# Seven block products per pair of weight units in the output and down projections of a transformer-style layer

## The chip, the cores and the metric

The kernel runs on one core of a Trainium2 chip. The core's engines work side by side: TensorE (PE, with PEld for its weight loads), VectorE (DVE), ScalarE (ACT), GpSimd (POOL) and SyncE (SP, which issues the DMAs). The time is that of one execution in device microseconds; a profile of one execution is read beside it.

## What is computed

One layer of a hybrid encoder runs over 512 prompt tokens and 32 sample tokens (544 in all, T in the code), model width 1024. Cut to the part that matters here:

```python
gate_a, gate_b = jnp.split(jax.nn.sigmoid(gates + b_gate), 2, axis=-1)
x = x + (gate_a * (ya @ w_proj_a) + gate_b * (yb @ w_proj_b)) @ w_out
u = rmsnorm(x, g_ffn) @ w_up                       # 1024 -> 2 x 3072
ug, uv = jnp.split(causal_dwconv(u_ext, ffn_conv_w, ffn_conv_b), 2, axis=-1)
x = x + (jax.nn.gelu(ug, approximate=True) * uv) @ w_down      # 3072 -> 1024
x = x + jax.nn.sigmoid(rmsnorm(x, g_ple) @ w_ple_gate) * (pe @ w_ple)
```

## The kernel before, in words

Activations lie with features on the 128 partitions and the 544 tokens along the row. All dense products run as one list of steps (`dense_steps`); TensorE takes them in exactly that order, since `Ordered` ties each matmul to the one before. The other engines' queues are ordered by the framework's scheduler.

A **unit** is a weight block of 1024 inputs by 128 outputs, 192 of them. Two units come in one 1 MB DMA (`load`, a ring of two buffers `wr`). `prep` splits a unit for the matmul: ACT rounds it to `wh` (L250), DVE subtracts to get the rest `wl` (L254; POOL does it for some of the first 40 units). Activations are split in the same way into `hi` and `lo`. A **chunk** (`mm3`) is one of a unit's eight input blocks: wh by hi, wh by lo, wl by hi, each on both halves of 272 tokens, 6 matmuls. A unit is 48 matmuls. Its result lies in a pair of PSUM banks (`dps`, two such pairs), and an epilogue on DVE and ACT takes it away.

The steps from the end of the gates on: `pb` (8 results of two units, the second branch), `out` (8 units), `up` in three parts of 16 units, `down` in three parts of 8 units, `pw` (8 small products), `gate` (8 units). The order is up, up, down, up, down, down, pw, gate. `ep_out` adds a unit's product to the residual `x[m]` on DVE (L1011), splits the sum for the next step (`split_g`, L374, L375) and adds its squares to `acc` (`add_sq`, L383, L384); `ep_down` does so too in the last part. From `acc`, `sum_parts` (L388, L389) and `rstd_of` make the norm's factor: matmuls `rps` with a matrix of ones, put off by some chunks (`defer`), then ACT. `conv_up` is the epilogue of an `up` unit: three DVE evictions, one ACT and two DVE operations, and two tiny POOL copies; `ep_uv` multiplies the two halves into `me` and splits it.

Matmuls, DVE and ACT operations appear under a helper's line (L130 for every matmul).

## Time and profile before

| | us |
|---|---|
| median of 3 runs | 1357.71 (1355.65 to 1357.8) |
| profiled execution, its own time | 1355.77 |
| span of its trace | 1354.1 |

The span is the time from the first to the last instruction; 1.7 us of the execution lie around it. Busy time of an engine includes the time in which an instruction has been started and is held up.

### The profile page before, as it was taken

To read this page: it belongs to the slowest core of one execution; us is meant where nothing else is said; L and a number is where in the kernel's file an instruction comes from. 1 tells how busy PE (TensorE), PEld (TensorE's weight loads), DVE (VectorE), ACT (ScalarE), POOL (GpSimd) and SP (SyncE) were. 2 spreads that over 40 slices of the span, in tenths; PEclk is the share of its full clock that TensorE was granted. 3 is DMA by queue.
4 is the path that set the end of the run, shared out by engine and by line. 5 is a ranking of instruction groups with operands and counts; after the bars stand their busy time and mean duration, and the time that the engine had idled before them with its cause. 6 is when DMAs were issued, how large, how long until landed. Compare 5 with 4: busy or idle time off the path is not lost.

```text
span 1354.1 us, 26563 instructions
## 1 busy us (share of the span) xinstructions
PE 1338.2 (99%) x11045; PEld 1307.2 (97%) x11045; DVE 852.6 (63%) x1474; ACT 634.4 (47%) x1104; POOL 313.7 (23%) x442
## 2 busy tenths in 40 slices
PE   8999999999999999999999999999999999999998
PEld 7999998999999999999999999999999999999998
DVE  7999889755775656643554335677676356753545
ACT  5465555656676667542442223534444124432342
POOL 5456365544321211100000000133332013310000
PEclk9999999999999999999999999999999999999999
DMA  5733243332533332222223422222222232222231
GB/s 182 252 100 130 83 128 121 119 132 100 177 94 114 115 111 90 67 81 94 69 89 110 143 94 73 85 94 94 94 72 85 94 111 94 76 85 94 94 107 53
DMA packets 41896, 142.15 MB, mean 105 GB/s; under 512 B 9216, under 2 KB 13232, under 8 KB 29488
## 3 DMA queue, kind: packets, MB, share of 16 engines
q1 hardware_dynamic: 41776, 140.45, 31.4%
q8 instruction: 87, 1.43, 0.4%
q14 instruction: 33, 0.27, 0.1%
HBM read 129.27 MB, written 14.31 MB: 106 GB/s over the span
## 4 chain that ended last, share of the span: by engine, by line
PE 89%; DVE 6%; ACT 2%; DMA 1%; issue 1%; SPq 0%; POOL 0%; ACTq 0%; DVEq 0%; POOLq 0%
PE dps L130 80%; PE O L130 2%; PE yps L130 2%; PE L L130 1%; PE st L130 1%; DVE cv L599 1%; DVE qs L834 1%; PE Tp L133 1%; DVE wl L254 1%; PE xst L133 0%; PE gps L130 0%; DMA wr<-in_w 0%; DVE xs L603 0%; DMA ab<-asc 0%; PE qn L130 0%
## 5 line engine op out<-in xcount | busy, mean ns | idle before, releaser
L130 PE MATMUL dps<-hi,wh 128*128 128x272 f32 x2960 | 627.0, 293 | 0.6 <-DVE ext L574 0.4
L130 PE MATMUL dps<-lo,wh 128*128 128x272 f32 x2960 | 613.1, 288 | 4.1 <-DVE lo L375 4.1
L130 PE MATMUL dps<-hi,wl 128*128 128x272 f32 x2960 | 612.1, 288 | 0.0
L130 PEld LDWEIGHTS dps<-hi,wh 128*128 128x128 f32 x2960 | 466.0, 189 | 10.5 <-issue 7.8
L130 PEld LDWEIGHTS dps<-lo,wh 128*128 128x128 f32 x2960 | 465.9, 189 | 5.0 <-DVE lo L375 5.0
L130 PEld LDWEIGHTS dps<-hi,wl 128*128 128x128 f32 x2960 | 464.9, 188 | 0.0
L250 ACT CAST wh<-wr 128x1024 fp32r<-128x1024 f32 x192 | 201.2, 1048 | 386.0 <-PE dps L130 346.6
L254 DVE TENSOR_TENSOR wl<-wr,wh 128x1024 fp32r<-128x1024 f32 x173 | 213.6, 1235 | 47.6 <-ACT wh L250 42.3
L1033 DVE SCALAR_TENSOR_TENSOR ucv<-uext,vec,ucv 128x546 f32<-128x546 f32 x96 | 75.3, 784 | 4.4 <-ACT ucv L1030 2.7
L599 DVE SCALAR_TENSOR_TENSOR cv<-ext,hv,cv 128x547 f32<-128x547 f32 x72 | 71.0, 986 | 2.1 <-ACT cv L596 1.0
L1026 POOL COPY cfo<-uext 128x2 f32<-128x2 f32 x48 | 10.4, 217 | 261.7 <-DVE uext L573 261.7
L1023 POOL MEMSET uext<- 128x2 f32 x48 | 4.5, 95 | 278.7 <-issue 278.7
L1065 DVE TENSOR_TENSOR x<-x,dps 128x544 f32<-128x544 f32 x24 | 17.3, 721 | 78.0 <-PE dps L130 78.0
L571 DVE TENSOR_TENSOR uext<-dps,rstd 128x272 f32<-128x272 f32 x48 | 21.3, 443 | 63.0 <-PE dps L130 58.3
L785 DVE CUSTOM_DVE_ANT_0 P<-L,bias 128x128 f32<-128x128 f32 (+3 forms) x64 | 30.8, 481 | 46.1 <-PE L L130 41.6
L254 POOL TENSOR_TENSOR wl<-wr,wh 128x1024 fp32r<-128x1024 f32 x19 | 48.4, 2549 | 43.9 <-ACT wh L250 42.4
L1027 POOL COPY cfo<-uext 128x2 f32<-128x2 f32 x48 | 55.5, 1157 | 0.0
L787 ACT ACTIVATE P<-P,sm 128x128 f32<-128x128 f32 (+3 forms) x64 | 36.0, 562 | 26.8 <-DVE sm L785 26.4
L660 POOL TENSOR_TENSOR ab<-ab,bc 128x512 f32<-128x512 f32 (+1 forms) x28 | 37.0, 1325 | 40.7 <-ACT ab L659 40.7
L368 ACT CAST hi<-me 128x544 fp32r<-128x544 f32 x24 | 15.5, 647 | 61.9 <-DVE me L1051 61.9
L1030 ACT ACTIVATE ucv<-uext,vec 128x546 f32<-128x546 f32 x48 | 40.7, 847 | 7.2 <-DVE uext L574 2.6
L650 ACT ACTIVATE m<-ab,tm 128x128 f32<-128x128 f32 x128 | 40.8, 389 | 6.3 <-DMA ab<-asc 6.2
(243 smaller groups left out, 1548.9 us busy)
## 6 DMA issues: line engine op xcount, KB each, us to landing
wr<-in_w SPq DMA_DIRECT2D x96, 1024.0 KB, 4.9
ab<-asc SPq DMA_DIRECT2D x32, 256.0 KB, 5.1
bsc<-evec SPq DMA_DIRECT2D x16, 320.0 KB, 8.0
bias<-bsc SPq DMA_DIRECT2D x16, 256.0 KB, 3.2
xin<-in_xT SPq DMA_DIRECT2D x8, 272.0 KB, 5.7
out_o_v<-v SPq DMA_DIRECT2D x8, 272.0 KB, 3.2
out_o_k<-qk SPq DMA_DIRECT2D x8, 272.0 KB, 2.9
x<-in_xT SPq DMA_DIRECT2D x8, 272.0 KB, 4.4
```

The source lines that it names most:

```text
L130: return self._pin(nc.tensor.matmul(*args, **kw))
L250: cp = S.copy(hi, r)
L254: eng.tensor_tensor(lo, r, hi.bitcast(F32), op=SUB)
L571: V.tensor_tensor(ext[:, n : n + HALF], ps[:, 0, :HALF], rstd[:, 0:HALF], op=MUL)
L599: V.scalar_tensor_tensor(y[:, :n], ext[:, j : j + n], hv[:, 24 * j + ti : 24 * j + ti + 1], y[:, :n], op0=MUL, op1=ADD)
L650: S.activation(m[:, i], ab[:Q, i], AF.Relu, scale=-1.0, bias=tm[:Q, 1, c, hd : hd + 1])
L660: G.tensor_tensor(ab, ab, cc[:, tk].unsqueeze(1).to_broadcast([128, H, Q]), op=MUL)
L785: V.tensor_tensor_reduce(out=P, in0=L, in1=B, scale=1.0, scalar=3e38, op0=ADD, op1=MIN, accum_out=nm[:n])
L787: S.activation(P, P, AF.Exp, scale=-1.0, bias=nm[:n], accum_out=sm[:n])
L1027: G.tensor_copy(cfo[:, i, 2:4], ext[:, UW - 2 : UW])
L1030: S.activation(y[:, :n], ext[:, 0:n], AF.Identity, scale=vec[:, V_FW + i : V_FW + i + 1], bias=vec[:, V_FB + i : V_FB + i + 1])
L1033: V.scalar_tensor_tensor(y[:, :n], ext[:, j : j + n], vec[:, V_FW + 48 * j + i : V_FW + 48 * j + i + 1], y[:, :n], op0=MUL, op1=ADD)
```

## The change

The `out` step and each of the three `down` parts (8 units each) are computed in four **pairs** of units. For a pair, weights, activations and result are cut into 2 by 2 blocks: weights by even and odd input blocks and by unit, activations by even and odd input blocks and by token half. Instead of the 8 block products of a pair, 7 are made, of sums and differences of the blocks. A block product is 4 input blocks of 3 matmuls, 12 matmuls; a pair is 84 matmuls where it was 96.

- `split7` (for two activation tiles): four differences on POOL of 272 columns, and six splits on ACT and DVE.
- `weight_sums` (for a pair): four sums and differences on POOL of 512 columns, into tiles `ws`.
- `prep_to`: weights are split in halves of 512 columns (one product's weights), two products to a tile; the ring of `wh` and `wl` has three tiles (it had two) from `pb` on.
- `product_out`: takes a product from PSUM and adds it to the blocks of the result that need it: one ACT copy, seven DVE and four POOL operations of 272 columns for a pair. The additions of squares move from DVE to POOL.
- `product`: the matmuls of one product; products 1 and 2, 6 and 7, and 5 and 3 share a pair of banks each, product 4 has a bank of its own.
- `dense_steps`: down 0 stands after the first 18 units of up, down 1 after 34, and down 2 after `pw`, directly ahead of `gate`.
- The host packs the weights of `w_out` and `w_down` with even input blocks first.

```diff
--- before.py
+++ after.py
...
-    p += [("pb", m) for m in range(8)] + [("out", m) for m in range(8)]
-
-    def up(t):
-        return [(n, i) for i in range(8 * t, 8 * t + 8) for n in ("ug", "uv")]
-
-    def down(t):
-        return [("down", t, m) for m in range(8)]
-
-    p += up(0) + up(1) + down(0) + up(2) + down(1) + down(2)
-    p += [("pw", m) for m in range(8)] + [("gate", m) for m in range(8)]
+    p += [("pb", m) for m in range(8)] + [("out", 0)]
+
+    def up(a, b):
+        return [(n, i) for i in range(a, b) for n in ("ug", "uv")]
+
+    p += up(0, 9) + [("down", 0)] + up(9, 17) + [("down", 1)] + up(17, 24)
+    p += [("pw", m) for m in range(8)] + [("down", 2)] + [("gate", m) for m in range(8)]
     return p
+
+
+SEVEN = [(p, n) for n in range(4) for p in (1, 2, 6, 7, 5, 3, 4)]
+NEW = ("pb", 0)
...
+    def weight_sums(j):
+        r = raws[j].rearrange("p u (k c) -> p (u k) c", c=512)
+        s = sums[j] = [slot(name="ws") for _ in range(4)]
+        s1, s2, s3, s4 = (t[:, 0:512] for t in s)
+        G.tensor_tensor(s1, r[:, 2], r[:, 3], op=ADD)
+        G.tensor_tensor(s2, s1, r[:, 0], op=SUB)
+        G.tensor_tensor(s3, r[:, 0], r[:, 2], op=SUB)
+        G.tensor_tensor(s4, r[:, 1], s2, op=SUB)
+
+    def prep_to(n):
+        while len(prepped) < min(n, len(tiles)):
+            w = tiles[len(prepped)]
+            hi = pools["w2"].tile([128, 1024], F32R, tag="wh", name="wh", bufs=3)
+            lo = pools["w2"].tile([128, 1024], F32R, tag="wl", name="wl", bufs=3)
+            prepped.append((hi, lo))
+            if isinstance(w, int):
+                load(w // 2)
+                parts = [(None, None, slice(0, 1024), raws[w // 2][:, w % 2, :])]
+                load(w // 2 + 1)
+            else:
+                parts = []
+                for i, (p, j) in enumerate(w):
+                    load(j)
+                    if p == 1:
+                        weight_sums(j)
+                        if j - 1 not in sums:
+                            load(j + 1)
+                    r = raws[j].rearrange("p u (k c) -> p (u k) c", c=512)
+                    if p in (1, 2, 4):
+                        src = r[:, {1: 0, 2: 1, 4: 3}[p]]
+                    else:
+                        src = sums[j][{5: 0, 6: 1, 7: 2, 3: 3}[p]][:, 0:512]
+                    parts.append((p, j, slice(512 * i, 512 * i + 512), src))
+            for p, j, sl, src in parts:
+                S.copy(hi[:, sl], src)
+                V.tensor_tensor(lo[:, sl], src, hi[:, sl].bitcast(F32), op=SUB)
+                if p == 4:
+                    load(j + 2)
+                if p == 3:
+                    done(*sums[j])
...
+        def product(self, st):
+            if self.cur is None:
+                kp = acts_of[st[0]](st)
+                head = [(i, (0, 1, 2)) for i in range(3)] + [(i, (3,)) for i in range(3)]
+                self.cur = [0, kp, head + [(i, (0, 1, 2, 3)) for i in range(3, 28)], at[0], {}]
+            n, kp, todo, t0, banks = self.cur
+            i, ks = todo[n]
+            if i == 0 and ks[0] == 0:
+                prep_to(t0 + 2)
+            elif i >= 3:
+                prep_to(t0 + i // 2 + 3)
+            wh, wl = prepped[t0 + i // 2]
+            p, q = SEVEN[i]
+            if ks[0] == 0:
+                j = i % 7
+                if j in (0, 2, 4):
+                    banks["d"] = dps()
+                banks[p] = sps("dpb")[:, :HALF] if j == 6 else banks["d"][:, j % 2, :HALF]
+            b = banks[p]
+            for k in ks:
+                o = 512 * (i % 2) + 128 * k
+                xh_, xl_ = kp[k][p]
+                for m, (w, x_) in enumerate(((wh, xh_), (wh, xl_), (wl, xh_))):
+                    PE.matmul(b, lhsT=w[:, o : o + 128], rhs=x_, start=k == m == 0, stop=k == 3 and m == 2)
+            self.count += len(ks) / 2
+            if ks[-1] == 3:
+                product_out(st, p, q, b)
+            self.cur[0] += 1
+            if self.cur[0] == len(todo):
+                at[0] = t0 + 14
+                pos[0] += 8
+                self.cur = None
+                self.i += 1
+                epilogue[st[0]](*st[1:])
...
+    def split7(t0, t1, g=None):
+        ta, tb = eslot("ta"), eslot("tb")
+        b11, b12, b21, b22 = (t[:, s] for t in (t0, t1) for s in (slice(0, HALF), slice(HALF, T)))
+        c1, c2, c3, c4 = (t[:, s] for t in (ta, tb) for s in (slice(0, HALF), slice(HALF, T)))
+        G.tensor_tensor(c1, b12, b11, op=SUB)
+        G.tensor_tensor(c2, b22, c1, op=SUB)
+        G.tensor_tensor(c3, b22, b12, op=SUB)
+        G.tensor_tensor(c4, b21, c2, op=SUB)
+        ts = [slot(F32R, n) for n in ("bh", "bh", "bh", "bl", "bl", "bl", "bx")]
+        h = [t[:, s] for t in ts for s in (slice(0, HALF), slice(HALF, T))]
+        res = {1: (h[0], h[6]), 2: (h[1], h[7]), 3: (h[2], h[8]), 4: (h[3], h[9]), 5: (h[4], h[10]),
+               6: (h[5], h[11]), 7: (h[12], h[13]), 0: ts}
+        for hi, lo, src in ((*res[1], b11), (*res[2], b21), (ts[2], ts[5], ta[:, :T]), (*res[7], c3),
+                            (*res[3], b22), (*res[4], c4)):
+            if g is None:
+                S.copy(hi, src)
+                V.tensor_tensor(lo, src, hi.bitcast(F32), op=SUB)
+            else:
+                S.activation(hi, src, AF.Copy, scale=g)
+                V.scalar_tensor_tensor(lo, src, g, hi.bitcast(F32), op0=MUL, op1=SUB)
+        return res
...
-    def ep_out(ps, m):
-        V.tensor_tensor(h2(x[m]), h2(x[m]), pv(ps), op=ADD)
-        xh.append(split_g(x[m], vec[:, V_GFFN + m : V_GFFN + m + 1]))
-        add_sq(acc, x[m], m == 0, V)
-        if m == 7:
-            for p in mh:
-                done(*p)
-            sp2 = sum_parts(acc)
-            dense.defer(7, lambda: rstd_of(rstd, sp2, 1.0 / D, tanhs))
+    tmp = []
+
+    def product_out(st, p, q, b):
+        x11, x12, x21, x22 = (x[m][:, s] for m in (2 * q, 2 * q + 1) for s in (slice(0, HALF), slice(HALF, T)))
+
+        def add(eng, to, y):
+            eng.tensor_tensor(to, to, y, op=ADD)
+
+        if p == 1:
+            tmp[:] = slot(name="su"), slot(name="sv")
+            s1 = tmp[0][:, 0:HALF]
+            S.copy(s1, b)
+            add(G, x11, s1)
+        elif p == 2:
+            add(V, x11, b)
+        elif p == 6:
+            u = tmp[0][:, HALF:T]
+            V.tensor_tensor(u, tmp[0][:, 0:HALF], b, op=ADD)
+            add(G, x21, u)
+        elif p == 7:
+            add(V, x21, b)
+            add(V, x22, b)
+        elif p == 5:
+            v = tmp[1][:, 0:HALF]
+            V.tensor_tensor(v, tmp[0][:, HALF:T], b, op=ADD)
+            add(G, x22, v)
+            add(G, x12, v)
+            done(*tmp)
+        elif p == 3:
+            add(V, x12, b)
+        else:
+            add(V, x21, b)
+        if p == 4 and st != ("down", 0) and st != ("down", 1):
+            dst, v = (xh, V_GFFN) if st[0] == "out" else (xp, V_GPLE)
+            for m in (2 * q, 2 * q + 1):
+                dst.append(split_g(x[m], vec[:, v + m : v + m + 1]))
+                add_sq(acc, x[m], m == 0, G)
+
+    def ep_out(_):
+        for p in mh:
+            done(*p[0])
+        sp2 = sum_parts(acc)
+        dense.defer(7, lambda: rstd_of(rstd, sp2, 1.0 / D, tanhs))
...
+        if i % 2:
+            mid7[i // 2] = split7(mid[i - 1], me)
+            done(mid[i - 1], me)
...
+    def ep_down(t):
+        for i in range(4 * t, 4 * t + 4):
+            done(*mid7[i][0])
         if t == 2:
-            xp.append(split_g(x[m], vec[:, V_GPLE + m : V_GPLE + m + 1]))
-            add_sq(acc, x[m], m == 0, V)
-        if m == 7:
-            for i in range(8 * t, 8 * t + 8):
-                done(*mid[i])
+            sp2 = sum_parts(acc)
+            dense.defer(4, lambda: rstd_of(rstd, sp2, 1.0 / D, gelus))
```

How the queues change, at three places. POOL, from the end of the attention stage to the first `up` unit: before, nothing of the output projection is on this engine (`klz` and `acc` belong to the attention stage, `uext` and `cfo` to the first `up` unit).

```order
L835 TENSOR_TENSOR klz1_4430<-qk_6834,ks1_7346 64x512
L384 TENSOR_TENSOR acc_130<-acc_130,sq_7370 128x544
L384 TENSOR_TENSOR acc_130<-acc_130,sq_7482 128x544
L1023 MEMSET uext_10593 128x2
L1024 COPY uext_10593<-ctx_f_107 128x2
L1026 COPY cfo_109<-uext_10593 128x2
L1027 COPY cfo_109<-uext_10593 128x2
```

Now, inside the output projection, from the first pair's additions to the second pair's (`x_10109` and `x_10111` are the first pair's results, `su` and `sv` the shared sums, `ws` the third pair's weight sums, `wr` its raw weights):

```order
L1151 TENSOR_TENSOR x_10109<-x_10109,su_10157 128x272
L1151 TENSOR_TENSOR x_10111<-x_10111,su_10157 128x272
L1151 TENSOR_TENSOR x_10111<-x_10111,sv_10158 128x272
L1151 TENSOR_TENSOR x_10109<-x_10109,sv_10158 128x272
L267 TENSOR_TENSOR ws_10328<-wr_10188 128x512
L269 TENSOR_TENSOR ws_10330<-wr_10188 128x512
L268 TENSOR_TENSOR ws_10329<-ws_10328,wr_10188 128x512
L270 TENSOR_TENSOR ws_10331<-wr_10188,ws_10329 128x512
L515 TENSOR_TENSOR acc_133<-acc_133,sq_10270 128x544
L1151 TENSOR_TENSOR x_10113<-x_10113,su_10286 128x272
L1151 TENSOR_TENSOR x_10115<-x_10115,su_10286 128x272
L267 TENSOR_TENSOR ws_10455<-wr_10296 128x512
```

Between one pair's additions there now stand the four weight sums of the pair after next and the additions of squares. DVE in the output projection before: an eviction, the next unit's weight rest, the split, the squares.

```order
L1011 TENSOR_TENSOR x_10017<-x_10017,dps_10090 128x544
L254 TENSOR_TENSOR wl_10155<-wr_9959,wh_10154 128x1024
L375 SCALAR_TENSOR_TENSOR lo_10147<-x_10017,vec_76,hi_10146 128x544
L384 TENSOR_TENSOR acc_130<-acc_130,sq_10150 128x544
L1011 TENSOR_TENSOR x_10019<-x_10019,dps_10153 128x544
L254 TENSOR_TENSOR wl_10216<-wr_10095,wh_10215 128x1024
L375 SCALAR_TENSOR_TENSOR lo_10208<-x_10019,vec_76,hi_10207 128x544
L384 TENSOR_TENSOR acc_130<-acc_130,sq_10211 128x544
```

DVE now, from the last eviction of the first pair into the second pair (`dps` and `dpb` are products in PSUM):

```order
L1151 TENSOR_TENSOR x_10111<-x_10111,dpb_10247 128x272
L484 SCALAR_TENSOR_TENSOR lo_10262<-x_10109,vec_79,hi_10261 128x544
L484 SCALAR_TENSOR_TENSOR lo_10267<-x_10111,vec_79,hi_10266 128x544
L298 TENSOR_TENSOR wl_10291<-ws_10181,wh_10290 128x512
L298 TENSOR_TENSOR wl_10291<-wr_9974,wh_10290 128x512
L1151 TENSOR_TENSOR x_10113<-x_10113,dps_10273 128x272
L1162 TENSOR_TENSOR su_10286<-su_10286,dps_10311 128x272
L298 TENSOR_TENSOR wl_10327<-wr_10188,wh_10326 128x512 x2
L1151 TENSOR_TENSOR x_10115<-x_10115,dps_10311 128x272 x2
L1169 TENSOR_TENSOR sv_10287<-su_10286,dps_10354 128x272
L298 TENSOR_TENSOR wl_10371<-ws_10329,wh_10370 128x512
L298 TENSOR_TENSOR wl_10371<-ws_10330,wh_10370 128x512
```

Behind the last eviction of a pair stand the splits of its two results, which need POOL's additions, and behind these the next pair's weights and evictions. TensorE, where the norm's factor is made for `gate`, before (`dps_15421` is the first `gate` unit; `down` ended 16 chunks of `pw` earlier):

```order
L130 MATMUL dps_15421<-hi_15024,wh_15355 128x272 x2
L130 MATMUL dps_15421<-lo_15025,wh_15355 128x272 x2
L130 MATMUL dps_15421<-hi_15024,wl_15356 128x272 x2
L130 MATMUL rps_15451<-ah_15306,ones_r_190 128x272
L130 MATMUL rps_15451<-al_15307,ones_r_190 128x272
L130 MATMUL rps_15455<-ah_15306,ones_r_190 128x272
L130 MATMUL rps_15455<-al_15307,ones_r_190 128x272
L130 MATMUL dps_15421<-hi_15085,wh_15355 128x272 x2
L130 MATMUL dps_15421<-lo_15086,wh_15355 128x272 x2
```

and now (`dps_16075` is the first `gate` unit, whose first 12 rows, four chunks, follow the last product of down 2; its last three rows ahead of `rps` and the first behind are shown):

```order
L145 MATMUL dps_16075<-hi_15782,wh_15992 128x272 x2
L145 MATMUL dps_16075<-lo_15783,wh_15992 128x272 x2
L145 MATMUL dps_16075<-hi_15782,wl_15993 128x272 x2
L145 MATMUL rps_16107<-ah_16071,ones_r_193 128x272
L145 MATMUL rps_16107<-al_16072,ones_r_193 128x272
L145 MATMUL rps_16111<-ah_16071,ones_r_193 128x272
L145 MATMUL rps_16111<-al_16072,ones_r_193 128x272
L145 MATMUL dps_16075<-hi_15925,wh_15992 128x272 x2
```

The four `rps` matmuls now stand four chunks behind the last product of `down`, and the sums that they read come from that product. Of the weight sums, those of a stage's first two pairs stand in POOL's queue ahead of the stage, those of the other two within it.

## Rows read from the trace of the kernel before

**Rows 1.** The page's first part: busy us (share of the span) xinstructions.

```profile
PE 1338.2 (99%) x11045; PEld 1307.2 (97%) x11045; DVE 852.6 (63%) x1474; ACT 634.4 (47%) x1104; POOL 313.7 (23%) x442
```

**Rows 2.** Windows: us, then PE, PEld, DVE, ACT, POOL busy; clock, DMA, GB/s.

```profile
100.00:200.00 100.00, 100.00 (x871) 93.75 (x870) 89.05 (x159) 57.31 (x118) 52.58 (x61) 1.00 0.35 110
805.50:853.50 48.00, 48.00 (x386) 48.00 (x385) 25.53 (x31) 17.45 (x23) 0.23 (x2) 1.00 0.26 88
850.00:1050.00 200.00, 200.00 (x1594) 200.00 (x1593) 141.16 (x243) 86.39 (x104) 61.26 (x128) 1.00 0.25 85
1237.40:1285.50 48.10, 48.10 (x386) 48.10 (x385) 23.92 (x29) 16.90 (x22) 0.00 (x0) 1.00 0.26 88
```

**Rows 3.** Tile view of x, 800 to 860 us: min/median/max ns, first, last start.

```profile
L1011 DVE TENSOR_TENSOR x<-x,dps x8: 720/721/722, 811.7 to 853.7; 128x544 f32<-128x544 f32 x8
```

**Rows 4.** DVE by form, 800 to 1060 us: busy us, mean ns, idle.

```profile
L254 DVE TENSOR_TENSOR wl<-wr,wh 128x1024 fp32r<-128x1024 f32 x43 | 52.7, 1225 | 6.7 <-ACT wh L250 5.6
...
L571 DVE TENSOR_TENSOR uext<-dps,rstd 128x272 f32<-128x272 f32 x32 | 14.2, 444 | 38.7 <-PE dps L130 35.0 <-ACT rstd L409 1.8
...
L1050 DVE TENSOR_TENSOR me<-ucv 128x512 f32<-128x512 f32 x16 | 11.1, 692 | 0.5
L375 DVE SCALAR_TENSOR_TENSOR lo<-x,vec,hi 128x544 fp32r<-128x544 f32 x8 | 6.2, 778 | 0.0
...
L389 DVE TENSOR_TENSOR al<-acc,ah 128x544 fp32r<-128x544 f32 x1 | 0.7, 726 | 0.7 <-ACT ah L388 0.7
```

**Rows 5.** ACT by form, 800 to 1056 us: busy us, mean ns, idle.

```profile
L250 ACT CAST wh<-wr 128x1024 fp32r<-128x1024 f32 x43 | 45.2, 1051 | 72.0 <-PE dps L130 60.8 <-issue 11.2
...
L374 ACT ACTIVATE hi<-x,vec 128x544 fp32r<-128x544 f32 x8 | 6.0, 752 | 0.0
L383 ACT ACTIVATE sq<-x 128x544 f32<-128x544 f32 x7 | 4.5, 642 | 0.0
...
L409 ACT ACTIVATE rstd<-rstd 128x272 f32<-128x272 f32 x2 | 0.9, 434 | 0.0
...
L388 ACT CAST ah<-acc 128x544 fp32r<-128x544 f32 x1 | 0.6, 648 | 1.4 <-DVE acc L384 1.4
```

**Rows 6.** Tile views of acc and ab: POOL operations, min/median/max ns.

```profile
L384 POOL TENSOR_TENSOR acc<-acc,sq x15: 1337/1357/2353, 172.0 to 559.2; 128x544 f32<-128x544 f32 x15
...
L660 POOL TENSOR_TENSOR ab<-ab,bc x26: 732/1292/1781, 80.6 to 317.1; 128x512 f32<-128x512 f32 x22, 128x256 f32<-128x256 f32 x4
```

**Rows 7.** Timeline 143.5 to 146.5 us: start us, duration us, engine, line.

```profile
143.80 1.20 DVE L254 TENSOR_TENSOR wl<-wr,wh 128x1024 fp32r<-128x1024 f32 x1
...
143.97 1.63 POOL L660 TENSOR_TENSOR ab<-ab,bc 128x256 f32<-128x256 f32 x1 [1.12 <-ACT ab L659]
...
144.93 1.25 DVE L599 SCALAR_TENSOR_TENSOR cv<-ext,hv,cv 128x547 f32<-128x547 f32 x1
```

**Rows 8.** Timeline, 253 to 256 us.

```profile
253.37 0.72 DVE L717 TENSOR_TENSOR z<-dps,rstd 128x544 f32<-128x544 f32 x1 [0.63 <-PE dps L130]
...
253.82 1.36 POOL L384 TENSOR_TENSOR acc<-acc,sq 128x544 f32<-128x544 f32 x1
...
254.20 2.06 DVE L254 TENSOR_TENSOR wl<-wr,wh 128x1024 fp32r<-128x1024 f32 x1
```

**Rows 9.** Timeline, 270 to 273 us.

```profile
270.40 1.21 DVE L254 TENSOR_TENSOR wl<-wr,wh 128x1024 fp32r<-128x1024 f32 x1
...
270.48 2.35 POOL L384 TENSOR_TENSOR acc<-acc,sq 128x544 f32<-128x544 f32 x1
```

**Rows 10.** Timeline, 64 to 66.5 us.

```profile
64.62 1.04 POOL L699 TENSOR_TENSOR h<-h,el 128x512 f32<-128x512 f32 x1 [4.01 <-ACT el L528]
...
65.22 0.99 DVE L603 SCALAR_TENSOR_TENSOR xs<-th,cv 128x512 f32<-128x512 f32 x1
```

**Rows 11.** Timeline of PE near the start.

```profile
16.15 0.55 PE L130 MATMUL dps<-lo,wh 128*128 128x272 f32 x2 [3.27 <-DVE lo L375]
```

**Rows 12.** Windows, 16.5 to 19.9 us.

```profile
16.50:19.90 3.40, 3.40 (x18) 3.40 (x16) 3.40 (x7) 0.61 (x2) 2.49 (x3) 0.50 0.99 380
```

More of the change, by code (lines that the diff above doesn't have):

```diff
@@ L88, in units_of @@
     if k == "out":
-        return [("w_out", 0, 128 * st[1])]
+        return [("w_out", 0, 128 * m) for m in range(8)]
     if k == "ug":
@@ L94, in units_of @@
     if k == "down":
-        return [("w_down", 8 * st[1], 128 * st[2])]
+        return [("w_down", 8 * st[1], 128 * m) for m in range(8)]
     if k == "pw" and st[1] % 4 == 0:
@@ L104, in unit_order, with tile_order @@
     return [u for st in dense_steps() for u in units_of(st)]
+def tile_order():
+    u, out, go = 0, [], False
+    for st in dense_steps():
+        go = go or st == NEW
+        us = units_of(st)
+        if st[0] in ("out", "down"):
+            assert u % 2 == 0
+            out += [[(p, u // 2 + n) for p, n in SEVEN[i : i + 2]] for i in range(0, len(SEVEN), 2)]
+        elif go:
+            out += [u + i for i in range(len(us))]
+        u += len(us)
+    return out
 V_GMIX, V_GSSM, V_GFFN, V_GPLE = 0, 8, 24, 32
@@ L314, in chunk @@
             st = self.steps[self.i]
+            if st[0] in ("out", "down"):
+                self.product(st)
+                return
             if self.cur is None:
@@ L1055, in ep_uv @@
                 done(*p)
+            nc.sync.dma_start(a["o_cf"], cfo)
+        if i == 20:
             for k in range(2):
@@ L1083, in acts_pw @@
         return ph
-    parts = []
     def ep_pw(ps, m):
@@ L1090, in ep_pw @@
         pw.append(t)
-        if m == 0:
-            parts.append(sum_parts(acc))
         if m == 7:
-            dense.defer(4, lambda: rstd_of(rstd, parts[0], 1.0 / D, gelus))
+            for p in ph:
+                done(*p)
     def ep_final(ps, m):
@@ L1126, in trunk @@
         "pa": acts_pa, "pb": acts_pb, "out": acts_out, "pw": acts_pw, "gate": lambda st: xp,
-        "down": lambda st: [mid[8 * st[1] + i] for i in range(8)],
+        "down": lambda st: [mid7[4 * st[1] + i] for i in range(4)],
     })
```

58 lines of the change are left out of this document (39 added, 19 removed).

## The prediction

> **What bounds the kernel now.** The page first: TensorE is busy 99% of the span, DVE 63%, ACT 47%, POOL 23% [rows 1]. Shares over a whole span hide the stages, so the windows come next: in the output projection and in the last down part TensorE is busy in all of the time at a granted clock of 1.00, DVE in about half, POOL in none [rows 2]. Then the pace: the eight evictions of the output projection start from 811.7 to 853.7, seven units in 42.0 us [rows 3], so a unit is 6.00 us and one of its 48 matmuls 0.125 us. TensorE waits for nobody there; a matmul taken out is worth 0.125 us as long as the other engines keep up. Whether they do is the question, since the change gives them more work and TensorE less time.
>
> **What is removed.** 32 units are 16 pairs; each loses 12 matmuls, 192 x 0.125 = 24.0 us. A pair takes 84 x 0.125 = 10.5 us, a stage of four pairs 42.0 where it was 48.0.
>
> The Trainium skill (TensorE: Matmul & The Clock Gate, Back-to-back issue gap) puts the distance of warm matmuls at N/2.4 + 2.5 ns, 116 ns for 272 columns; by that the gain would be 22.2 us. The trace has 125 ns, and that is used.
>
> **What is added, engine by engine.** Prices [rows 4 to 6]. DVE: 272 columns out of PSUM 0.44 us, 512 columns 0.69, a scaled split of 544 columns 0.78, a whole unit's rest 1.23. ACT: 272 columns 0.43, a scaled copy of 544 0.75, a square 0.64, a unit's cast 1.05. POOL has no operation of 272 columns in this trace; undisturbed it takes 0.73 for 256 and 1.36 for 544 (lowest of the one, median of the other row of [rows 6]), so 0.77 for 272 and 1.29 for 512.
> One stage of `out` (from the last product of `pb` to its own last product), counted in the queues:
> - ACT: 28 half casts (half of 1.05 and some start, 0.6), 4 copies, 8 scaled copies, 8 squares, 3 casts for the next step, splits left over: some 36 us of 42. It fits.
> - DVE: 28 evictions, 12.3; 24 half rests, 16.6; six scaled splits, 4.7; the last addition of `pb` and its split, 3.2; three rests for `up`, 3.7. 40.5 us of 42: full, though a next operation starts some 0.07 us before the end of the last.
> - POOL: 3 differences and 16 additions of 272 columns, 14.6; 8 weight sums (those of the first two pairs are made in `pb`), 10.3; five additions of squares, 6.8. 31.7 us.
> Each would just fit alone. They aren't alone.
>
> **DVE and POOL hold each other up.** At 143.80 a DVE rest starts; POOL's operation of 256 columns, started 0.17 later, ends 0.60 behind it, at 145.60; the DVE operation started at 144.93 ends 0.58 behind that, at 146.18, where one of 544 columns takes 0.78 alone [rows 4, 7]. At 254.20 a rest waits for POOL and takes 2.06 instead of 1.23, ending 1.08 behind POOL's end [rows 8]; at 270.48 POOL waits for a rest and ends 1.22 behind it [rows 9]; a DVE operation of 512 columns ends 0.55 behind POOL's [rows 10]. The evictions, which read PSUM, run beside POOL undisturbed: the product taken at 253.37 took its 0.72 [rows 8]. So a DVE operation with both inputs in SBUF and a POOL operation take turns, and in a turn directly behind the other engine they cost (their held time) DVE 0.55 (512), 0.58 (544), 1.08 (1024), 0.30 (272, by the slope), POOL 0.63 (272, by the slope from 256 to 544), 1.15 (512), 1.22 (544). The sum of the turns is a bound on a stage that no single engine's busy time shows:
> - `out`: POOL 19 x 0.63 + 8 x 1.15 + 5 x 1.22 = 27.3; DVE 24 x 0.55 + 7 x 0.58 + 4 x 0.30 + 0.58 + 3 x 1.08 = 22.3. Together 49.6 for 42.0: 7.6 us too much.
> - down 2, without the differences and the split ahead: POOL 16 x 0.63 + 8 x 1.15 + 5 x 1.22 = 25.4, DVE 22 x 0.55 + 6 x 0.58 + 3 x 1.08 = 18.8, 44.2: 2.2 too much.
> - down 0 and down 1, without squares and splits of `x`, but with the epilogue of the unit before: POOL 19.3, DVE 22 x 0.55 + 3 x 1.08 + 2 x 0.58 + 0.55 = 17.1, 36.4. They fit.
> These are the low bounds of the lock. The high ones take each operation at its full duration: 59.9, 53.0 and twice 43.9, 17.9 + 11.0 + 3.8 = 32.7 too much. Where both queues are full they alternate, as in rows 7, so I take the held times.
>
> **The ends.** Behind the last product come an eviction 0.44, a scaled copy 0.75, a square 0.64, POOL's addition 1.36, a cast 0.65 and a rest 0.73 [rows 4 to 6], 4.6 us, before the `rps` matmuls can run. In `out` seven chunks of 0.75 us stand ahead of them, 5.25, which cover this and 0.7 of the lag. At down 2 only four chunks do, 3.0: 1.6 us are open that were hidden behind `pw` before. So `out` loses 6.9, down 2 loses 3.8.
>
> **Bursts.** Between two evictions DVE has up to two operations that may each wait for a turn of POOL: 2 x (1.15 + 0.55) + 0.44 = 3.8 us, where TensorE takes that pair of banks again after two products, 3.0. Up to 0.8 us for a pair, between 0 and 16 x 0.8 = 13; the later pairs' sums, whose weights are loaded within the stage, make one such pair in each stage likely. I charge one pair in four, 4 x 0.84 = 3.4 us.
>
> **What I cost at nothing.** The `up` units. In the windows DVE is busy 141.16 of 200 us [rows 2], 4.2 of a unit's 6.0; the finer splits add a quarter of 5 x 0.44 + 0.73 against half of 0.73, 0.4, and a quarter of four differences makes DVE wait 0.6: 5.2 of 6.0, hidden behind TensorE's own matmuls. The eight weight sums ahead of a down part lie on about five units and take turns of 9.2 us more, 7.1 a unit: DVE falls some 5 us behind, where two pairs of banks let it be a unit late, 6.0. If this cover is gone it costs up to 4 us ahead of each of the three parts. The loads of `x` stood between the weight loads of `pb`; now SP issues them from the beginning of the last `pb` result on, some 10 us before the first is needed.
>
> **Sum.** 24.0 - 6.9 - 3.8 - 3.4 = 9.9 us faster: 1355.8 - 9.9 = 1345.9 against the profiled execution's own time. That lies 1.9 below the median of the three runs, so I say 1347, between the two. What a measurement of this kernel can tell from no change is some 0.2%, 2.7 us.
>
> **Rivals.**
> - *All of it is hidden.* For it: POOL's operations in `out` can slip past the stage's end, and from 100 to 200 us DVE was busy 89% and POOL 53% and TensorE 100% [rows 2]. Against: the splits that the next step needs stand behind them. It leaves the 1.6 at the end of down 2: 1333.4.
> - *Slower: the lock at full durations*, in the four stages. It decides against the change from a mean of 12.0 us a pair instead of 10.5; the held times give 11.1 on average (177.8 / 16), the full ones 12.5 (200.7 / 16). Then the loss is 32.7 - 0.7 + 1.6 = 33.6, and the time 1365.4. For it: a blocked operation that starts late also pushes the evictions behind it on DVE. Against: rows 7 to 10 show the starts overlapping every time. The Trainium skill (SBUF — State Buffer, Who interferes with whom) states this rival as its rule: whoever issues first has the shared pair of ports for the whole instruction, and the other blocks fully. By that rule it would be 1365.4; the trace agrees that one waits, but the waiting one ends 0.1 to 0.2 us sooner than its full duration behind the other.
> - *The clock falls.* At 16.15 us TensorE went on after a wait of 3.3 us [rows 11]; from 16.5 to 19.9 its granted clock was 0.50, the 1.2 GHz level, and 18 matmuls started there [rows 12] where 27 would at 0.125. Waits of that length at the ends of `out` and down 2 or within them would cost 1.2 us each time; three to six of them give 1350 to 1354. Against: weights that come late split the wait into small ones.
> - *The change doesn't do what it says* is excluded: TensorE's queue has 192 matmuls fewer.
>
> **How the numbers follow.** My forecast (1340 to 1353) 0.50, all hidden (1333 to 1340) 0.17, the full lock (1354 to 1366) 0.22, the clock 0.08, else 0.03. Without the ends of these the range is 1334 to 1362. Faster: forecast, hidden, and most of the clock, 0.72; within 0.2% 0.11; slower 0.17.
>
> **What would show it.** In the profile after: TensorE at 125 ns wherever it runs; waits of TensorE for `wl` and the splits of `x` in `out`, about twice as much as in down 2, and little in down 0 and 1; POOL's 512-column sums at 1.2 to 1.9 us and half rests above 0.69. Wrong it would be if TensorE waited mainly in `up` (then the sums ahead of the parts are the cost), for a DMA of `wr` or `x`, or if DVE's rests beside POOL kept 0.69.

## The result and the profile after

The change makes the kernel slower: 1441.48 us (1440.23 to 1443.69, 4 runs) against 1357.44 of the kernel before on the same chip, a ratio of 1.0624 with a 95% interval of 1.0605 to 1.0642. That is 84 us more, where 10 fewer were predicted, and 76 above the slowest time that any rival of the prediction gave. The span of the profiled execution is 1438.7 us.

The page's first part after, which answers to [rows 1]:

```profile
PE 1351.3 (94%) x10853; PEld 1307.8 (91%) x10853; DVE 1004.8 (70%) x1684; ACT 685.4 (48%) x1264; POOL 543.9 (38%) x648
```

192 matmuls fewer, as counted, and TensorE no longer at 99%. Windows of the four stages, from the first matmul of a stage to the first behind it (columns as in [rows 2]): the output projection, down 0, down 1, down 2.

```profile
805.55:872.40 66.85, 50.98 (x339) 48.02 (x337) 50.26 (x66) 26.37 (x48) 38.62 (x32) 0.90 0.20 65
983.45:1046.10 62.65, 48.48 (x338) 45.67 (x337) 43.73 (x66) 19.47 (x35) 30.99 (x34) 0.95 0.21 70
1143.07:1206.20 63.13, 50.62 (x338) 47.62 (x337) 43.37 (x66) 20.32 (x36) 31.88 (x35) 0.89 0.22 73
1314.95:1379.90 64.95, 48.71 (x338) 45.99 (x337) 44.74 (x59) 24.79 (x44) 35.61 (x29) 0.92 0.20 67
```

Each stage should take 42.0 us and took 63 to 67. Of the 84 us, 65.6 lie here (257.6 us where the four stages took 192) and 12.8 between down 1 and down 2 (1206.20 to 1314.95, where 14 units of `up` and `pw` took 96.0 at the old pace). The loss is nearly the same in all four, though squares and splits of `x` are made in two of them only. No engine but TensorE is busy for more than 50.3 of these us, so no engine's load alone explains them. The next view is what TensorE waits for, from 800 us on (engine, line, what it waited for: us in total, times, longest):

```profile
PE dps L145 <- ACT su L1156: 27.8, 16, 4.9
PE dps L145 <- DVE su L1162: 13.9, 16, 2.1
PE dps L145 <- DVE sv L1169: 10.7, 16, 1.0
PE dps L145 <- ACT pw L1259: 9.5, 1, 9.5
PE dps L145 <- DVE uext L705: 5.6, 2, 2.9
PE rps L145 <- ACT ah L519: 3.1, 2, 2.5
PE rps L145 <- DVE al L520: 0.7, 2, 0.4
...
```

The first three rows are the finding. There are 16 pairs of units, and each of the three evictions L1156 (product 1), L1162 (product 6) and L1169 (product 5) is waited for 16 times: 48 waits, 52.4 us. The timeline shows who waits (start, duration, engine, line; in brackets the idle time before and what ended it):

```profile
998.41 0.68 DVE L298 TENSOR_TENSOR wl<-ws,wh 128x512 fp32r<-128x512 f32 x1
999.01 0.43 DVE L1169 TENSOR_TENSOR sv<-su,dps 128x272 f32<-128x272 f32 x1
...
999.50 0.39 PE L145 MATMUL dps<-bh,wh 128*128 128x272 f32 x1 [0.85 <-DVE sv L1169]
...
1000.97 1.30 POOL L267 TENSOR_TENSOR ws<-wr 128x512 f32<-128x512 f32 x1
...
1001.83 2.69 DVE L298 TENSOR_TENSOR wl<-ws,wh 128x512 fp32r<-128x512 f32 x2
...
1002.23 1.74 POOL L269 TENSOR_TENSOR ws<-wr 128x512 f32<-128x512 f32 x1
...
1004.16 0.62 ACT L297 CAST wh<-ws 128x512 fp32r<-128x512 f32 x1 [1.85 <-PE dps L145]
1004.69 0.61 ACT L297 CAST wh<-wr 128x512 fp32r<-128x512 f32 x1
1005.21 0.38 ACT L1156 COPY su<-dps 128x272 f32<-128x272 f32 x1
...
1005.64 0.39 PE L145 MATMUL dps<-bh,wh 128*128 128x272 f32 x1 [1.39 <-ACT su L1156]
```

At 999.50 product 3 begins. Its own bank has long been free; but it shares the two-bank tile with product 5, and its first matmul waits until product 5's eviction (999.01 to 999.44) is through. At 1005.64 product 2 does the same behind product 1. The trace's semaphores say so too: the matmul at 999.50 waits for one semaphore, VectorE's, and the one at 1005.64 for one, ScalarE's, and in each pair the first matmul of products 2, 7 and 3 is released by the eviction of products 1, 6 and 5. The program makes it wait for the tile as one thing, though the two products lie in different banks of it. So TensorE stands still for a whole eviction three times in a pair, and longer when the eviction is queued: at 999.01 behind a half rest, at 1005.21 behind two casts, which themselves had waited for TensorE to leave a weight tile.

### The profile page after: what moved, and what is told of

Read it like the earlier page. It is cut to its first block, busy times and chain, and to the rows that moved or that the text cites. A ratio compares the mean times of both kernels' runs of the same rounds, so it can differ in the third digit from the quotient of the medians.

```text
span 1438.7 us, 26855 instructions
## 1 busy us (share of the span) xinstructions
PE 1351.3 (94%) x10853; PEld 1307.8 (91%) x10853; DVE 1004.8 (70%) x1684; ACT 685.4 (48%) x1264; POOL 543.9 (38%) x648
## 5 line engine op out<-in xcount | busy, mean ns | idle before, releaser
L145 PE MATMUL dps<-hi,wh 128*128 128x272 f32 x2576 | 548.1, 294 | 9.9 <-ACT pw L1259 9.5
L145 PE MATMUL dps<-lo,wh 128*128 128x272 f32 x2576 | 537.3, 290 | 4.2 <-DVE lo L484 4.2
L145 PE MATMUL dps<-hi,wl 128*128 128x272 f32 x2576 | 535.1, 289 | 0.0
L145 PEld LDWEIGHTS dps<-hi,wh 128*128 128x128 f32 x2576 | 408.0, 189 | 19.9 <-ACT pw L1259 9.9
L297 ACT CAST wh<-wr 128x1024 fp32r<-128x1024 f32 (+1 forms) x122 | 105.4, 877 | 190.1 <-PE dps L145 167.2
L298 DVE TENSOR_TENSOR wl<-wr,wh 128x1024 fp32r<-128x1024 f32 (+1 forms) x122 | 136.7, 1131 | 25.8 <-ACT wh L297 25.2
L145 PE MATMUL dps<-bh,wh 128*128 128x272 f32 x320 | 101.5, 317 | 44.2 <-ACT su L1156 27.8
L317 ACT CAST wh<-wr 128x1024 fp32r<-128x1024 f32 x86 | 89.7, 1043 | 102.5 <-PE dps L145 99.2
L145 PE MATMUL dps<-bl,wh 128*128 128x272 f32 x320 | 97.3, 304 | 0.7 <-DVE bl L506 0.7
L145 PE MATMUL dps<-bh,wl 128*128 128x272 f32 x320 | 96.8, 303 | 0.0
L321 DVE TENSOR_TENSOR wl<-wr,wh 128x1024 fp32r<-128x1024 f32 x67 | 84.5, 1262 | 6.3 <-ACT wh L317 3.6
L298 DVE TENSOR_TENSOR wl<-ws,wh 128x512 fp32r<-128x512 f32 x64 | 64.6, 1039 | 15.7 <-ACT wh L297 15.3
```

Of the source, the lines that this page charges most:

```text
L145: return self._pin(nc.tensor.matmul(*args, **kw))
L297: S.copy(hi[:, sl], src)
L298: V.tensor_tensor(lo[:, sl], src, hi[:, sl].bitcast(F32), op=SUB)
L317: cp = S.copy(hi, r)
L321: eng.tensor_tensor(lo, r, hi.bitcast(F32), op=SUB)
```

## The experiments

All times are medians, each beside runs of the kernel before on the same chip; its medians there were 1356.3 to 1357.1, and 1357.44 beside the changed kernel. So a difference between runs of two chips is uncertain by about 1 us. Windows and waits are those of one profiled execution of each run.

**Own tiles: take the shared tile away.** Products 1, 6 and 5 take a `dps` tile each, the others a one-bank tile.

```diff
-                if j in (0, 2, 4):
-                    banks["d"] = dps()
-                banks[p] = sps("dpb")[:, :HALF] if j == 6 else banks["d"][:, j % 2, :HALF]
+                banks[p] = dps()[:, 0, :HALF] if j in (0, 2, 4) else sps("dpb")[:, :HALF]
```

> The changed kernel with one edit: each of the seven products has a PSUM tile of its own (two tiles of tag d, four of tag s), where products 1 and 2, 6 and 7, 5 and 3 shared a two-bank tile. Theory A, the shared tile: the first matmul of the second product of a tile waits for the eviction of the first (48 waits), and these waits with the clock that falls in them are most of the loss. Then the four stages, now 66.8, 62.6, 63.1 and 64.9 us, fall to 42 to 50 us each and the time from 1441.5 to 1350 to 1375 us. Theory B, the turns of VectorE and GpSimd set the pace of the stages, whatever the banks: the stages stay above 58 us, the time above 1420. Theory C, only the granted clock is at fault and would fall from any wait: stages 55 to 60 us, time 1400 to 1420.

Measured: 1389.46 us, ratio 1.0242 (1.0213 to 1.0271), 52.0 less than the changed kernel (50.9 by what each lost to the kernel before beside it). Windows of its four stages, and its waits for the norm:

```profile
808.70:861.10 52.40, 45.31 (x339) 44.00 (x338) 51.17 (x65) 25.96 (x47) 42.40 (x32) 0.97 0.23 79
977.00:1023.40 46.40, 43.62 (x338) 43.43 (x336) 41.29 (x64) 20.00 (x36) 32.95 (x33) 0.96 0.25 83
1120.40:1166.80 46.40, 43.64 (x338) 43.45 (x338) 41.27 (x64) 19.90 (x36) 32.96 (x33) 0.96 0.28 89
1275.50:1325.20 49.70, 43.94 (x339) 42.42 (x338) 44.08 (x54) 24.18 (x43) 35.98 (x27) 1.00 0.21 68
```

```profile
PE rps L145 <- ACT ah L517: 9.3, 2, 6.4
```

The stages fell by 62.7 us together, from 257.6 to 194.9; some 9 us came back behind the output projection and down 2, where the waits for the norm grew from 3.8 to 9.6 us (9.3 of them for L517). Another 3.2 us are lost ahead of the output projection, which the edit does not touch. The 48 waits are gone: what is left of waits for the three evictions is 7.0 us in five. The stages lie in theory A's 42 to 50 us but for the output projection, and the time ended 14 us above theory A's range, so the tile is not all.

**No weight sums: take GpSimd's largest part away.** Products 5, 6, 7 and 3 read raw weight blocks; the tiles stay shared.

```diff
-        s = sums[j] = [slot(name="ws") for _ in range(4)]
-        s1, s2, s3, s4 = (t[:, 0:512] for t in s)
-        G.tensor_tensor(s1, r[:, 2], r[:, 3], op=ADD)
...
+        sums[j] = [r[:, i] for i in (3, 0, 2, 1)]
...
```

> The changed kernel without the 64 weight sums on GpSimd: products 5, 6, 7 and 3 take raw weight blocks in their place, so the output is not the reference's; shared tiles as in the changed kernel. Theory A: the waits on the shared tile stay and are only shortened where the eviction stood behind a held half rest; 1415 to 1435 us, stages 58 to 64 us. Theory B (turns): 8 sums of 1.15 us a stage are gone from a stage that they set the pace of, 9 to 10 us in each, and with them waits and clock: 1400 us or less, stages 50 to 55 us.

Measured: 1405.84 us, ratio 1.0359 (1.033 to 1.0387), 35.6 less than the changed kernel. That is between the two theories, 5.8 above B's 1400 and 9.2 below A's range, and the stages (61.0, 54.6, 54.6, 58.7 us) are A's in two and B's in two. They make 28.7 of the gain. Neither theory had seen that the sums also cost something outside the stages: the wait in `pw`, below, is 0.5 us here where it was 9.5. In the other direction, this execution came to the output projection 6.0 us later (811.50 against 805.55), in a stretch that the edit leaves alone.

**Both.**

> Both edits, own tiles and no weight sums on GpSimd (output not the reference's). Theory A with the turns as predicted: with own tiles the turns are what is left, 2 x 9.2 us over capacity at most in the output projection and in the last down part, so this gains 5 to 12 us over own tiles alone. Theory B: 1380 us, as in the run without sums and 20 or more below own tiles alone.

Measured: 1356.80 us, ratio 1.000 (0.9989 to 1.0011). The two edits nearly add up: 52.0 and 35.6 apart, 84.7 together. The gain of the second over own tiles alone is 32.7 where theory A had 5 to 12, and theory B had 1380 us. So theory A and theory B are each a part of the story. Windows of the four stages, and what TensorE waited for longest:

```profile
806.40:851.55 45.15, 42.91 (x338) 42.28 (x337) 43.29 (x62) 26.06 (x47) 25.41 (x22) 1.00 0.26 83
968.70:1010.85 42.15, 42.15 (x338) 42.15 (x337) 33.68 (x60) 18.38 (x33) 17.97 (x20) 1.00 0.30 101
1108.10:1150.35 42.25, 42.25 (x338) 42.25 (x337) 34.54 (x61) 18.94 (x34) 17.44 (x20) 1.00 0.33 107
1248.40:1291.80 43.40, 42.46 (x337) 42.10 (x337) 37.74 (x55) 24.39 (x43) 22.01 (x19) 1.00 0.24 80
```

```profile
PE rps L145 <- ACT ah L510: 10.0, 2, 6.6
```

Here the stages are what the seven products promise, 173.0 us for 192, and yet the kernel is only level with the one before. The rest went at the ends: from 851.55 to 968.70 lie 18 units of `up` and four short matmuls, 108.5 us at the old pace, which took 117.15; and from 1291.80 to the end of the span, 1355.0, it took 63.2 us, where `gate` and what follows it took 56.6 before (12 us of `pw` behind 1285.5 of [rows 2], to 1354.1).

**The order alone.** The kernel before, with plain products and the new order of steps.

```diff
-    p += up(0) + up(1) + down(0) + up(2) + down(1) + down(2)
-    p += [("pw", m) for m in range(8)] + [("gate", m) for m in range(8)]
+    p += up(0, 9) + down(0) + up(9, 17) + down(1) + up(17, 24)
+    p += [("pw", m) for m in range(8)] + down(2) + [("gate", m) for m in range(8)]
...
```

The lines left out put the norm's sums behind down 2, as in the changed kernel.

> The kernel before with the new order of steps alone (down parts after 18 and 34 units of up, the last one behind pw, the norm's matmuls four chunks behind it); plain products, ring of two. Theory A: the order costs little in itself; what it costs is a wait in pw, whose copies stand on ScalarE behind the split of the last up unit, and the open end at down 2 of 1 to 3 us: 1358 to 1368 us. Rival D, the order is a main cost: 1380 us or more.

Measured: 1358.95 us, ratio 1.0019 (1.0009 to 1.0028). The order costs 2.6 us, 1.6 of it waits for the norm behind down 2. There is no wait in `pw`, which the expectation had, so the 9.5 us there are not the order's. The run with own tiles shows whose they are; its timeline:

```profile
1258.86 1.22 POOL L489 TENSOR_TENSOR ta<-me 128x272 f32<-128x272 f32 x1
1260.04 1.56 POOL L268 TENSOR_TENSOR ws<-ws,wr 128x512 f32<-128x512 f32 x1
1261.56 0.95 POOL L490 TENSOR_TENSOR ta<-me,ta 128x272 f32<-128x272 f32 x1
...
1262.55 0.65 ACT L500 CAST bh<-ta 128x544 fp32r<-128x544 f32 x1 [1.97 <-POOL ta L490]
...
1263.59 0.60 ACT L1257 COPY pw<-dps 128x544 f32<-128x544 f32 x1
...
1264.25 0.82 PE L145 MATMUL dps<-hi,wh 128*128 128x272 f32 x2 [9.46 <-ACT pw L1257]
```

The third `pw` product needs the first one's banks. Its copy stands on ACT behind the casts of the last `split7`, these wait for GpSimd's differences, and GpSimd makes weight sums for down 2 ahead of them and in between (1254.82 to 1258.15, and from 1260.04).

**Weight sums on VectorE.** Own tiles, and `G.tensor_tensor` becomes `V.tensor_tensor` in the four lines of `weight_sums`.

> Own tiles as in the first run, and the 64 weight sums moved from GpSimd to VectorE. Theory T, turns: a sum on GpSimd costs VectorE a held rest and GpSimd a late addition; on VectorE it costs its own 0.69 us alone. VectorE was busy 43.3, 33.7, 34.6 and 37.7 us in the four stages without sums, with 8 x 0.69 = 5.5 us more it is 39 to 49: stages of 47 to 49 us in the output projection and 42 to 46 in the down parts, the wait of 9.5 us in pw gone as without sums, 1362 to 1370 us. Rival U, VectorE's own load is the limit in the stages: moving work onto it makes the stages longer than the 52.3, 46.5, 46.4 and 49.7 us of own tiles alone, time above 1389.

Measured: 1370.91 us, ratio 1.0108 (1.0093 to 1.0124), 18.6 less than with the sums on GpSimd; down 0 and 1 took 42.85 us each, the output projection 50.75, down 2 47.65. Every stage is shorter than with own tiles alone, which rules out rival U. Of theory T's figures, those of down 0 and 1 came; the output projection and down 2 are 1.7 above theirs, and the time 0.9. The wait in `pw`, which should be gone, stayed at 7.8: now the four sums stand on VectorE (1240.93 to 1245.33) ahead of the multiplication that the last `split7` reads (1246.06).

**The norm put off.** In the next three kernels the first unit behind the norm takes the older factor, since its own comes after that unit's eviction; this part of the computation is changed in them, and it makes them a measure of the ends and no version.

```diff
-        dense.defer(7, lambda: rstd_of(rstd, sp2, 1.0 / D, tanhs))
+        dense.defer(13, lambda: rstd_of(rstd, sp2, 1.0 / D, tanhs))
...
-            dense.defer(4, lambda: rstd_of(rstd, sp2, 1.0 / D, gelus))
+            dense.defer(13, lambda: rstd_of(rstd, sp2, 1.0 / D, gelus))
```

> Own tiles as in the first run, and the four matmuls of the norm's factor put off by 13 chunks behind the output projection and behind down 2, where it was 7 and 4. In the run with own tiles TensorE waited 9.3 us for the last sums of squares there, at two places, and ran on at the lower clock. If that is the open end, both waits go: 9 to 13 us less than own tiles alone, 1376 to 1381 us. If the wait only moves to the eviction of the next units (the factor is needed there), less than 4 us.

> Own tiles, weight sums on VectorE, the norm's matmuls 13 chunks behind, and the additions of product 5 of a stage's last pair on VectorE. Theory T and the open ends together: 1348 to 1358 us, the first version that may be level with or ahead of the kernel before (1356.3). Theory U: above 1375.

> Own tiles, no weight sums at all (raw blocks in their place, the output is not the reference's), the norm's matmuls 13 chunks behind. It asks where the rest of the 24 us went: without sums and with own tiles the stages took 45.1, 42.1, 42.2 and 43.5 us, 19 less than before, yet the time was that of before, since the two waits for the norm, the clock behind them and the rest lost 18. If these are the ends, 1342 to 1347 us. If they are something else, 1354 to 1358.

Measured: 1376.96, 1361.92 and 1352.47 us (ratios 1.0154, 1.0049 and 0.9972). With own tiles the two ends are worth 12.5 us, as expected; without sums only 4.3, a miss: TensorE then waits 5.1 us for splits of `x` (L475), four times. With the sums on VectorE the time is 3.9 us above the expected range, another miss: the wait in `pw` is still 7.9, and TensorE waits 7.0 us for two half rests (L298). So more than the norm's matmuls lies open there.

**All the rest of it, in a kernel that computes everything.** Own tiles, sums on VectorE, the norm seven chunks behind down 2 (the unit's eviction allows no more), product 5's additions of a stage's last pair on VectorE.

> The whole change (four stages by seven products) with own tiles, weight sums on VectorE, the norm's matmuls seven chunks behind down 2 (it was four) and product 5's additions of a stage's last pair on VectorE; nothing is left out. From the run with sums on VectorE: three chunks of 0.75 us at the end of down 2, and 2 to 5 us at the end of the output projection: 1362 to 1367 us. Below 1356 it would be a version of the whole change that pays; I give that 1 in 10.

Measured: 1369.20 us, ratio 1.0097 (1.0067 to 1.0127), above the range as a median; two of its four runs (1364.53 and 1365.95) lie in it, and the profiled one is the slowest, 1375.0. There the end, from the last product of down 2 on, is 3.75 us shorter (57.50 where it was 61.25), but down 1 took 47.20 instead of 42.85: at its head TensorE waited 3.3 us for the eviction of the last `up` unit on VectorE (L703). In the run with sums on VectorE that eviction stands in the same place of the queue, and TensorE waited 0.5. What differs is how long VectorE waited for weights ahead of its sums for down 1, 0.87 and then 0.23 us in that run, 3.23 and 1.20 in this one. The first sum there and here:

```profile
1088.74 0.69 DVE L267 TENSOR_TENSOR ws<-wr 128x512 f32<-128x512 f32 x1 [0.87 <-DMA wr<-in_w]
```

```profile
1092.50 0.69 DVE L267 TENSOR_TENSOR ws<-wr 128x512 f32<-128x512 f32 x1 [3.23 <-DMA wr<-in_w]
```

While the sum waits for the transfer, what stands behind it in VectorE's queue waits too, and the evictions stand there. That this is the whole loss is read from the queue and was not tried apart, and how often it happens in the other three runs is not shown. Of the versions that compute everything, none with all four stages paid.

**Seven products in down 0 and down 1 alone.** There lie no norm and no `pw` beside them. The output projection and down 2 are as in the kernel before, own tiles, sums on VectorE. Three versions that differ in one edit each: as it is; shared tiles back; sums back on GpSimd.

> Seven products in down 0 and down 1 alone, own tiles, weight sums on VectorE; the output projection and the last down part by eight products as in the kernel before, and the last part ahead of pw again. In the run with sums on VectorE these two parts took 42.8 and 42.9 us where they took 48.0 before, while the output projection and down 2 with what follows them gained nothing (50.7 and 47.6 us, then the wait for the norm and the wait in pw). If the losses are bound to those two places: 2 x 5.1 less some 1 us, 1344 to 1349 us. If work added to VectorE is only paid elsewhere (in the up units that carry the sums), 1353 to 1358.

> The run before this one with the shared two-bank tiles put back: products 1 and 2, 6 and 7, 5 and 3 of a pair in one tile. That is 24 waits of TensorE for an eviction, with GpSimd nearly idle beside them. Theory A: without sums on GpSimd but with shared tiles the two parts took 54.6 us, 12.5 more than with own tiles; twice that, 20 to 27 us, so 1366 to 1374 us, slower than the kernel before by the tile alone. If the tile only hurts where GpSimd holds the evictions up, less than 8 us more than with own tiles.

> Seven products in down 0 and down 1 alone with own tiles, as in the run that was faster than the kernel before (1347.2 us), with the weight sums back on GpSimd. It is the cleanest price of the turns: one edit, no shared tile, no norm and no pw near. The prediction held that in these two parts the turns fit (36.4 of 42.0 us): then 1345 to 1349 us, no difference. By the four-stage run with own tiles, 46.4 us each instead of 42.9, they do not: 7 us more, 1352 to 1357.

Measured: 1347.19 us, ratio 0.9934 (0.9922 to 0.9947), faster than both kernels; 1382.39 us, ratio 1.019 (1.0174 to 1.0205); 1355.48 us, ratio 0.9991 (0.998 to 1.0002). Windows of the two parts, as it is:

```profile
964.55:1007.50 42.95, 42.37 (x338) 42.18 (x338) 40.27 (x72) 18.44 (x33) 20.40 (x19) 1.00 0.30 99
1104.10:1147.15 43.05, 42.35 (x339) 42.16 (x338) 42.01 (x72) 19.19 (x33) 19.49 (x19) 1.00 0.29 99
```

With the shared tiles, windows and then waits:

```profile
965.05:1027.60 62.55, 48.03 (x338) 45.19 (x337) 42.01 (x73) 18.81 (x33) 18.18 (x20) 0.95 0.22 70
1124.20:1182.20 58.00, 47.06 (x338) 44.26 (x337) 42.61 (x73) 19.14 (x33) 18.36 (x20) 0.97 0.24 78
```

```profile
PE dps L147 <- DVE sv L1173: 10.3, 8, 3.9
PE dps L147 <- ACT su L1160: 7.5, 8, 1.4
PE dps L147 <- DVE su L1166: 6.4, 8, 1.4
```

The shared tile alone, in eight pairs: 24 waits, 24.2 us of them, 35.2 us of time. VectorE is busy for 42.01 and 42.61 us where it was 40.27 and 42.01, in one operation more: the load is the same, and TensorE stands still beside it. The starts of the matmuls show where the other 11 us are. The two windows are 34.6 us longer: TensorE is idle for 24.2 us more, the first two steps from matmul to matmul at each wait are, idle time aside, 6.7 us longer than 0.125 each, and 35 other matmuls follow at over 0.17 us, 3.6 us more, which is the lower clock. The time is above its range. One wait alone is 3.9 us: product 5's eviction (978.70) stood on VectorE behind two sums, the first of which had waited 1.58 us for its weights (977.49). In the run without sums but with shared tiles no wait in these two parts is over 1.4.

With the sums on GpSimd the cost is 8.3 us (on another chip; 9.1 by what each gained on the kernel before beside it), in the second of the two expected ranges. TensorE waits mainly in one place per part:

```profile
PE dps L147 <- DVE uext L705: 4.9, 2, 2.9
```

That is the last `up` unit's eviction on VectorE, at the head of each part, while GpSimd makes sums; with the sums on VectorE this wait is 1.3 us. The windows of the two parts there:

```profile
964.90:1011.70 46.80, 43.85 (x338) 43.66 (x337) 41.80 (x65) 20.25 (x36) 33.11 (x34) 0.96 0.26 86
1108.30:1153.95 45.65, 43.03 (x339) 42.29 (x338) 41.77 (x64) 19.11 (x34) 33.11 (x32) 1.00 0.26 87
```

## Why the prediction was wrong

**The step that failed: Bursts.** It said that "TensorE takes that pair of banks again after two products, 3.0", and gave an eviction that long before anyone misses it; one pair in four would cost 0.84, 3.4 in all. The tile was asked for at once, by the second product in it. Three times in a pair TensorE waited for an eviction that it was meant to run beside. 48 waits of 1.09 us took the place of four stalls of 0.84; taking the shared tile out gave back 52.0 us, and putting it into eight pairs of a kernel that had none cost 35.2. The prediction went by the banks, and product 2 has one of its own; what its first matmul waits for follows from the tile, and that stands in the program and not in the profile of before. None of the rivals had this either: the result lay in the 0.03 that the prediction left for anything else.

**The turns of VectorE and GpSimd: the mechanism right, the size not.** Predicted 7.6 and 2.2 us over 42.0 in the output projection and in down 2, and a fit in down 0 and 1. With own tiles, where they can be seen: 10.4, 7.7, 4.4 and 4.4; without the sums 3.2, 1.4, 0.2 and 0.3. So of the 26.9 us over with own tiles, 22.0 go with the sums. I had charged a sum 1.15 and taken 1.29 as its undisturbed time. The tile view of `ws` in the changed kernel (min/median/max ns):

```profile
L298 DVE TENSOR_TENSOR wl<-ws,wh x64: 679/693/1845, 800.1 to 1367.5; 128x512 fp32r<-128x512 f32 x64
L267 POOL TENSOR_TENSOR ws<-wr x16: 1287/1316/1971, 782.3 to 1341.8; 128x512 f32<-128x512 f32 x16
L269 POOL TENSOR_TENSOR ws<-wr x16: 1737/1764/2266, 784.1 to 1343.2; 128x512 f32<-128x512 f32 x16
...
L270 POOL TENSOR_TENSOR ws<-wr,ws x16: 1260/1382/2281, 790.8 to 1347.6; 128x512 f32<-128x512 f32 x16
```

The lowest of 1.26 to 1.29 in three of the four sums bear out the 1.29 worked out from [rows 6]; the medians, with VectorE at work beside them, are 1.32 to 1.76. The half rests, which should be above 0.69, keep a median of 0.69 here, with single ones up to 1.85; with own tiles it is 0.90. The two half rests that took 2.69 us together, in the timeline above, are the lock of [rows 7 to 10] at work. So the rival "the lock at full durations", 32.7 us over the four stages, was nearer with own tiles than the forecast's 9.8. That all of the 22.0 are turns is not shown: without the sums, half rests also no longer wait for a sum to be made.

**A cost named at nothing that was one: the sums ahead of a part.** "If this cover is gone it costs up to 4 us ahead of each of the three parts": it is gone. In down 0 and 1 it is 3.9 and 2.6 us (46.80 and 45.65 us against 42.95 and 43.05 in the runs of two parts), with the wait at the head of each; ahead of down 2 the same sums hold up the last split and through it `pw`, 9.5 us, which is nowhere in the prediction.

**The ends.** Predicted 0.7 hidden behind the output projection and 1.6 open at down 2. In the changed kernel itself TensorE waits 3.8 us for the norm. Where the stages run at their pace it is more, 10.3 with own tiles and no sums, and 15 us with what follows (8.6 and 6.6): the chain was counted from an eviction that is not late, but in that run VectorE's last two additions of the output projection waited 1.4 us for GpSimd's additions of product 5, and started 3.5 us after the last product. The chain was also counted for one result, and a pair's last product brings two: the second one's split, square and addition (857.71 to 860.62) follow the first one's (855.57 to 858.35). From the last product to `rps` it took 9.8 us where 4.6 were counted.

**The clock.** As a rival it was priced at three to six waits of some 3 us. It did fall, and it is a part of the loss, not the cause. Two windows within down 1 of the changed kernel (us, PE busy, matmuls started, granted clock):

```profile
1147.40:1157.60 10.20, 8.36 (x34) 0.50 0.20 59
1160.00:1180.00 20.00, 17.07 (x130) 1.00 0.16 53
```

Of TensorE's two levels it ran 10 us at the lower, 1.2 GHz, and started 34 matmuls there, one in 0.30 us with its waits; at 2.4 GHz, also with waits, one in 0.15. The mean granted clocks of 0.89 to 0.95 in the stages make 44 us at the lower level in all. The starts of the matmuls give the price: of the 89.6 us that the four stages took over 4 x 42.0, TensorE was idle for 58.8, the first two steps at each wait cost 15.4 more, and the other steps of over 0.17 us, at the lower clock, 15.0 more.

This stretch of 10 us began in the wait of 2.8 us for the last `up` unit's eviction (until 1148.24), not in a wait for a shared tile. Of the nine falls of the clock in the four stages, eight came in a wait of 1.9 to 4.9 us or within 1.5 us behind one, where an eviction was late; the ninth came in a wait of 1.1 behind two shorter ones. In the run without sums but with shared tiles, down 0 and down 1 hold 24 waits for the shared tile, of 0.5 to 1.4 us, and the granted clock stays at 1.00:

```profile
983.60:1038.20 54.60, 45.27 (x338) 42.66 (x337) 34.65 (x61) 18.48 (x33) 16.65 (x20) 1.00 0.24 80
1135.50:1190.10 54.60, 45.30 (x338) 42.66 (x337) 35.37 (x62) 19.06 (x34) 16.66 (x20) 1.00 0.26 84
```

The Trainium skill (TensorE: Matmul & The Clock Gate, A second HAM failure mode: psum-queue depth-cycling) describes short idle times between groups of matmuls that make the clock go back and forth. In the changed kernel it does go between 0.50 and 1.00, mostly with its longer waits; these two parts have the short ones without it.

**What was right.** 192 matmuls fewer at 0.125 us: 42.15 us for a part where nothing waits. The `up` units away from the parts: 96.97 us from the end of down 0 to the start of down 1 (1046.10 to 1143.07), for 96.0. TensorE waits for no transfer in the stages. The Trainium skill's formula that the prediction sets beside the 125 ns (TensorE: Matmul & The Clock Gate, Back-to-back issue gap) is given there for an isolated matmul; the stream here has a weight load for every matmul. The test that the text set, waits in `out` "about twice as much as in down 2, and little in down 0 and 1", failed: the four windows are nearly equal, and what TensorE waits for is evictions. With own tiles the order is the predicted one (10.4, 7.7 and twice 4.4 us over).
